# Two blocks of an output projection put into a hand-written order on all queues, and two copies out of banks moved forward

## The chip, the core and the metric

The kernel runs on one core of one Trainium2 chip. It is one layer of a diffusion transformer, launched once. The metric is the device time of one launch in microseconds (us), lower is better. The time before is the median of three runs. In the text PE is the matrix engine, ACT the scalar engine, DVE the vector engine, POOL the engine that here adds squares and issues a few transfers, and SP the engine whose queue issues nearly all loads.

## What is computed

512 latent tokens and 256 context tokens of width 2048 pass one layer: modulated RMSNorm, one input projection, eight heads of differential attention and eight of latent attention, one output projection, and a gated MLP of width 5632 whose gate passes a convolution of width 3. What matters here, cut from the reference:

```python
mod_x = (silu(c) @ w_ada + b_ada)               # 6 x 2048 numbers for the whole sequence
sh1, s1, g1, sh2, s2, g2 = split(mod_x, 6)
x = x + g1 * (merge_heads(o_da, o_mla) @ w_o)    # output projection, 2048 x 2048
h2 = rmsnorm(x, norm2_w) * (1 + s2) + sh2
g, u = split(h2 @ w_up, 2)
x = x + g2 * ((silu(conv3(g)) * u) @ w_down)
return rmsnorm(x, final_w)
```

## The kernel before, in words

Everything is kept transposed: a tile has 128 features on the partitions and 512 tokens along the free axis. Products keep near float32 accuracy from fast matmuls by splitting each operand into a high and a low part. A weight block of 128x1024 is loaded by SP into a buffer `wr` (a ring of three). ACT casts it to the high part `wh` (line 250 in `split`, or line 1740 in `cast`), and DVE subtracts that from the raw block to get the low part `wl` (line 251, or line 1748 in `low`). `wh` and `wl` are rings of three as well. One product is then three matmuls (`mm3`, lines 286 to 288): high by high, high by low, low by high. The first two need only `wh`; the third needs `wl`.

**The output projection** makes 16 feature tiles in four groups of four. Each group runs over eight weight blocks `w_o[g, kb]`, and each block feeds 24 matmuls of 512 columns (`project`, line 1409). The four groups:

- Group 0 (the first block) belongs to an order of steps that a planner wrote for attention (`ATTENTION_ORDER`). It sums into two double banks `s`. One weight block of group 1 is prepared there too (`first_blocks`, line 1438).
- Groups 1 and 2 (the second and third block) are the loop of lines 1493 to 1511. It is written outside any hand-ordered region, so the framework's own scheduler decides the order on every queue. Group 1 sums into four banks `b`, group 2 into the double banks `s`.
- Group 3 is the list of jobs `("o", kb)` (`last_projection`, line 1770), inside a hand-ordered region. There PE, ACT, DVE and SP execute exactly in the order in which the program names their instructions.

When a group ends, each of its four sums is closed: DVE multiplies it by g1 and adds the residual (`gated`, line 1490; `residual`, line 1482, loads the residual tile `xr`, a ring of four, and reserves the result), POOL issues the write of the result to DRAM (line 1510), ACT squares it (line 1463 or 1466, `sq` with two buffers), and POOL adds the square to the running sum `ss` (line 1467), which the second RMSNorm needs. In a group's last weight block the matmuls are sorted by output, so that the four sums become complete one after the other.

**The late part of the modulation** is worked off beside the projection. 22 columns of `modx` are still to be made. For each, a row of 128x2048 floats (1 MB) of `w_ada` is loaded into `ada` (two buffers), and DVE multiplies it with silu(c), which lies broadcast in `cb`, and sums along the row (line 354 in `gemv`, line 1766 in `late_gate`; called a gate below). Sixteen gates belong to groups 1 and 2, one for each weight block; six belong to the jobs of group 3. `late_row` (line 1757) loads the row, `late_gate` works it off and calls `late_row` for the next one.

**After the projection** come the sum of squares over partitions (PE, lines 1823 and 1826 in `last_projection`) and the norm, then the up projection: three tiles computed plainly (jobs `n` and `u`) and 41 tiles by Strassen's method in seven products each (jobs `("p", ft, k)`, `product`, line 1929; the first such tile is ft = 3). Down projection blocks (`d`) are put between them later on. For every job i, `strassen` issues the matmuls, then `cast(i + 2)` on ACT, then `after(jobs[i - 1])`, then `low(i + 2)` on DVE.

In a Strassen tile the seven products are summed in three banks `y`, `z`, `x`. `y` is read in between: product 0 is copied out (`kept`, line 1682, an ACT copy into a ring `m` of two buffers; called m1), product 2 is then added in the same bank and copied as u2, and so is `z` after product 3 (m5). A product that adds to a bank has to wait until the copy of the bank's earlier state is done. `m` has two buffers, so m5 needs m1 to have been used up; that is done by the gate half's `put_together` (lines 1687 and 1688, DVE). In the tile before, the convolution (lines 1660 and 1662), Silu (line 1667), the product with u (line 1671) and the split into parts (lines 1673 and 1677) are finished during this tile's products.

Of the kernel before, what the change touches and what calls it, by code (L numbers as in the profile page):

```python
# [9 lines left out]
F32 = mybir.dt.float32  # L10
# [212 lines left out]
def layer_kernel(ctx: ExitStack, tc: tile.TileContext, small, rope, c_row, cc_row, x_t, ctx_t, ada, ada_k,  # L223
# [15 lines left out]
    def s_tile():  # L239
        return ps_s.tile([P, 1024], F32, tag="s", name=nm("s"))  # L240
# [3 lines left out]
    def b_tile(tag="b", bufs=None):  # L244
        return ps_b.tile([P, 512], F32, tag=tag, name=nm(tag), bufs=bufs or nb[0])
# [29 lines left out]
    def wblock(src):  # L275
        return wsplit(wload(src))
# [466 lines left out]
    def next_gemv(pool, count):  # L743
        for _ in range(count):
            j = next(gv, None)
            if j is not None:
                gemv(pool, j, [(cb, modx)])
# [661 lines left out]
    def project(outs, i, kt, w, stop=False):  # L1409
        o = (kt % 2) * 512 + i * P  # L1410
        mm3(outs[i], (w[0][:, o:o + P], w[1][:, o:o + P]), osp[kt], kt == 0, kt == 15 or stop)
# [44 lines left out]
    tp = tc.alloc_tile_pool(name="tp", bufs=8, reuse_waits="tile")  # L1456
    wo = tc.alloc_tile_pool(name="wo", bufs=1, reuse_waits="tile")
    cb = wo.tile([P, D], F32, name="cb2")
    nc.sync.dma_start(cb, silu_c.to_broadcast([P, D]))

    def add_square(pool, ss, x, first):
        if first:
            sc.square(ss, x)
        else:
            q = pool.tile([P, T], F32, tag="sq", name=nm("sq"), bufs=2)[:, :x.shape[1]]
            sc.square(q, x)
            gp.tensor_tensor(out=ss, in0=ss, in1=q, op=ALU.add)
# [14 lines left out]
    def residual(dt):  # L1482
        xr = wo.tile([P, T], F32, tag="xr", name=nm("xr"), bufs=4)
        nc.sync.dma_start(xr, x_t[dt])
        x1.append(b2k())
        return xr

    def gated(dt, po, xr, c=slice(0, T)):

        ve.scalar_tensor_tensor(out=x1[dt][:, c], in0=po[:, c], scalar=modx[:, 32 + dt:33 + dt], in1=xr[:, c],  # L1490
                                op0=ALU.mult, op1=ALU.add)

    for g in range(3):
        if g % 2:
            outs = [b_tile() for _ in range(4)]
        elif g:
            s0, s1 = s_tile(), s_tile()
            outs = [s0[:, :512], s0[:, 512:], s1[:, :512], s1[:, 512:]]
        else:
            outs = g0_outs  # L1500
        for kb in range(8 if g else 0):
            next_gemv(wo, 1)
            w = g1_first.pop(0) if g1_first else wblock(w_o[g, kb])
            order = [(j, i) for j in range(2) for i in range(4)]
            for j, i in sorted(order, key=lambda t: t[1]) if kb == 7 else order:
                project(outs, i, kb * 2 + j, w)
        for i in range(4):
            dt = g * 4 + i
            gated(dt, outs[i], residual(dt))
            gp.dma_start(x1_d[dt], x1[dt])  # L1510
            add_square(wo, ss, x1[dt], dt == 0)

    KBS = [kb for j in range(4) for kb in (j, j + 4)]
    jobs = [("o", kb) for kb in range(8)] + [("n", kb) for kb in KBS] + [("u", b) for b in range(4)]
# [157 lines left out]
    def kept(src):  # L1680
        t = mem["mm"].tile([P, T], F32, tag="m", name=nm("m"), bufs=2)
        sc.copy(t, src)
        return t
# [80 lines left out]
    def late_gate():  # L1764
# [2 lines left out]
                                scalar=col("b_ada", j), accum_out=modx[:, j:j + 1])  # L1767
        late_row()

    def last_projection(i):  # L1770
        kb, w = jobs[i][1], [h[0] for h in ready[i][:2]]
        if kb < 6:
# [169 lines left out]
    def output_block(c, w):  # L1942
        live["po"] = []
        for d in range(2):
# [2 lines left out]
                mm3(po, w[f * 2 + d], acts[c * FC + f], f == 0, f == FC - 1)  # L1947
            live["po"].append(po)

    def after(job):  # L1950

        if job == ("u", 3):
            live[2] = {"g": live["s"][0], "u": live["s"][1], "t": gate_in(2, live["s"][0])}
        elif job[0] == "d":
            for d, po in enumerate(live["po"]):
                dt = job[2] * 2 + d
                x = mem["mm"].tile([P, T], F32, tag="xs", name=nm("xs"), bufs=XS)
                sc.mul(x, po, modx[:, 80 + dt:81 + dt])  # L1958
                gp.dma_start(x1_d[dt], x, accum_op=ALU.add)  # L1959
        if job[0] != "p":  # L1960
            return
        ft, k = job[1:]
        v, f = live[ft], live.get(ft - 1)
        if k == 0:
            v["m1"] = kept(v["y"])
        elif k == 2:
            v["u2"] = kept(v["y"])
            if f:
                silu(convolve(ft - 1, f["g"], f["t"]))
        elif k == 3:  # L1970
            if f:
                acts[ft - 1] = multiply(f["t"], f["u"])
            v["g"] = mem["mm"].tile([P, T], F32, tag="g", name=nm("g"), bufs=1)
            put_together(v["g"][:, h0], v["x"], v["m1"])
            v["m5"] = kept(v["z"])
        elif k == 4:
            if f:
                finish(f["t"], acts[ft - 1])
            v["u"] = mem["mm"].tile([P, T], F32, tag="u", name=nm("u"), bufs=1)
            put_together(v["u"][:, h1], v["y"], v["m5"])  # L1980
        elif k == 5:
            put_together(v["u"][:, h0], v["z"], v["u2"])
        elif k == 6:
            v["t"] = gate_in(ft, v["g"])
# [8 lines left out]
    def strassen(i):  # L1993
        job = jobs[i]
        if job[0] == "p":
            ft, k = job[1:]
            product(ft, k, weights(i))
            if k in (1, 2) or (k == 0 and ft > 3):
                weight_sum(ft, k + 2)
            elif k == 6:  # L2000
                weight_sum(ft + 1, 1)
            if (ft, k) == (NFT - 1, 1):
                for dt in range(KT):
                    x1[dt] = a2k()
                    nc.sync.dma_start(x1[dt], x1_d[dt])
            if ft == 3 and k < 2:
                fill(len(queue) if k else 4)
        else:
            output_block(job[1], weights(i))
        second_gate(jobs[i - 1])  # L2010
        cast(i + 2)
        after(jobs[i - 1])
        low(i + 2)


# [106 lines left out]

    with tc.manual_schedule(engines={mybir.EngineType.PE, mybir.EngineType.Activation, mybir.EngineType.DVE,
                                     mybir.EngineType.SP}):
        mem["ra"] = Ring(wp, "wr", 3, items_a)
        live["o"] = [b_tile() for _ in range(4)]
        live["xr"] = [residual(12 + d) for d in range(4)]
        ve.tensor_tensor(db, modx[:, 56:64], modx[:, 48:56], op=ALU.add)
        late_row()
        late_row()  # L2130
        for i in range(2):
            cast(i)
            low(i)
        for i, job in enumerate(jobs):
            if job == ("n", 0):
                ps_b.release()
                ps_s.release()
                nb[0] = 3
                ps_b = tc.alloc_tile_pool(name="ps_m", bufs=3, space=PSUM, reuse_waits="tile")
                spare += [tp.tile([P, T], F32R, tag="tp", name=nm("tp")) for _ in range(8)]  # L2140
            {"o": last_projection, "n": first_tiles, "u": third_tile, "p": strassen, "d": strassen,
             "f": last_output}[job[0]](i)
# [86 lines left out]
```

## Time and profile before

| | |
|---|---|
| median of three runs | 2338.05 us (2332.84 to 2338.72) |
| profiled execution, its own time | 2336.14 us |
| its span, first to last instruction | 2334.4 us |
| PE busy | 2290.5 us (98%) |
| DVE busy | 1722.1 us (74%) |
| ACT busy | 1164.1 us (50%) |
| mean granted PE clock | 0.993 of full speed |

The profile is of one execution. A row of a timeline says when an instruction started, how long it took, engine, line, operation, what it writes and reads, and in brackets how long the engine sat idle before it and who released it. The row of a DMA on the SP queue is only its issue; landing is told by the views of transfers and of the chain of waits. A matmul of 512 columns is listed with about 0.39 us, but starts follow each other closer than that, since matmuls are pipelined; the distance of the starts is what counts.

### The profile page before, as it was taken

Reading aid. Unit: us, or ns where it says so; the run is one execution under the profiler, and the core shown is the slowest. Engines: PE = TensorE matmul, PEld = TensorE weight load, DVE = VectorE, ACT = ScalarE, POOL = GpSimd, SP = SyncE. Lnnn points to the kernel's source line nnn. Section 1 sums busy time; section 2 is a strip of 40 time slices with the busy share of each in tenths; the row PEclk is TensorE's granted clock in tenths of the full one; section 3 lists DMA queues with packets and bytes.
Section 4 is the critical chain, followed back from the end, with each engine's and each line's share of the span. In section 5 each row is a group of like instructions: output and inputs, shape, how many; then the busy total and the mean of one; then the engine's idle time right before and its main releaser. Section 6 shows DMA issues by size and latency. Waiting matters only on the chain.

```text
span 2334.4 us, 32178 instructions
## 1 busy us (share of the span) xinstructions
PE 2290.5 (98%) x12378; PEld 1960.0 (84%) x12378; DVE 1722.1 (74%) x2206; ACT 1164.1 (50%) x1777; POOL 266.2 (11%) x308
## 2 busy tenths in 40 slices
PE   6999999999999999999999999999999999999998
PEld 5788888888888878898888888888888888888887
DVE  7988785689877575897675858585858585867667
ACT  6542311577777522455454545454545454545455
POOL 0000001200133131000101010101010101010110
PEclk8999999999999999999999999999999999999999
DMA  9978888546210298434646473646464555555573
GB/s 367 370 254 306 302 305 298 168 135 203 81 34 28 93 353 293 155 120 129 140 137 151 111 169 109 171 111 155 132 147 130 139 136 144 136 146 125 156 184 103
DMA packets 124731, 404.23 MB, mean 173 GB/s; under 512 B 14337, under 2 KB 18945, under 8 KB 114081
## 3 DMA queue, kind: packets, MB, share of 16 engines
q1 hardware_dynamic: 96658, 346.92, 44.4%
q0 software_dynamic: 26768, 54.21, 12.6%
q8 instruction: 97, 1.59, 0.3%
q10 hardware_dynamic: 1152, 1.05, 0.1%
q14 instruction: 56, 0.46, 0.1%
HBM read 332.45 MB, written 69.67 MB: 172 GB/s over the span
## 4 chain that ended last, share of the span: by engine, by line
PE 90%; DMA 4%; DVE 3%; issue 1%; ACT 1%; SPq 0%; POOL 0%; DVEq 0%; ACTq 0%; POOLq 0%
PE y L1938 13%; PE b L286 10%; PE b L287 9%; PE b L288 9%; PE y L1940 7%; PE z L1938 6%; PE s L1025 4%; PE z L1940 3%; PE s L286 3%; PE s L288 3%; PE x L1938 3%; PE s L287 3%; DMA ada<-in_ada 2%; PE pt L1045 2%; PE f L286 2%; PE f L288 2%
## 5 line engine op out<-in xcount | busy, mean ns | idle before, releaser
L1748 DVE TENSOR_TENSOR wl<-wr,wh 128x1024 fp32r<-128x1024 f32 x144 | 176.5, 1226 | 139.5 <-ACT wh L1740 138.8
L1959 POOL DMA_DIRECT2D x_d<-xs x160 | 139.6, 993 | 1148.3 <-ACT xs L1958 1146.3
L1740 ACT CAST wh<-wr 128x1024 fp32r<-128x1024 f32 x144 | 150.9, 1048 | 218.4 <-PE b L287 113.2
L286 PE MATMUL b<-ah,wh 128*128 128x512 f32 (+1 forms) x664 | 256.8, 387 | 0.0
L287 PE MATMUL b<-al,wh 128*128 128x512 f32 (+1 forms) x664 | 256.7, 387 | 0.0
L288 PE MATMUL b<-ah,wl 128*128 128x512 f32 (+1 forms) x664 | 255.8, 385 | 0.0
L1748 DVE TENSOR_TENSOR wl<-rb,wh 128x1024 fp32r<-128x1024 f32 x123 | 150.0, 1220 | 120.7 <-ACT wh L1740 120.7
L1748 DVE TENSOR_TENSOR wl<-ws,wh 128x1024 fp32r<-128x1024 f32 x123 | 150.3, 1222 | 110.1 <-ACT wh L1740 110.1
L1740 ACT CAST wh<-rb 128x1024 fp32r<-128x1024 f32 x123 | 129.3, 1051 | 175.1 <-PE b L287 80.1
L1938 PE MATMUL y<-a2k,wh 128*128 128x512 f32 x656 | 164.0, 392 | 0.0
L1740 ACT CAST wh<-ws 128x1024 fp32r<-128x1024 f32 x123 | 128.4, 1044 | 69.7 <-PE b L287 44.1
L288 PEld LDWEIGHTS b<-ah,wl 128*128 128x128 f32 x664 | 124.8, 188 | 25.7
L286 PEld LDWEIGHTS b<-ah,wh 128*128 128x128 f32 x664 | 125.1, 188 | 22.9
L287 PEld LDWEIGHTS b<-al,wh 128*128 128x128 f32 x664 | 125.1, 188 | 21.9
L250 ACT CAST wh<-wr 128x1024 fp32r<-128x1024 f32 x51 | 53.5, 1052 | 171.6 <-DMA wr<-in_w_o 45.2
L1938 PEld LDWEIGHTS y<-a2k,wh 128*128 128x128 f32 x656 | 118.6, 189 | 21.6
L354 DVE CUSTOM_DVE_ANT_0 ada<-ada,cb,smt 128x2048 f32<-128x2048 f32 x37 | 88.2, 2388 | 30.3 <-DMA ada<-in_ada 30.1
L1938 PE MATMUL y<-b2k,wh 128*128 128x512 f32 x410 | 106.8, 390 | 0.0
L1958 ACT ACTIVATE xs<-b,modx 128x512 f32<-128x512 f32 x160 | 101.7, 681 | 6.2 <-DMA x_d<-xs 6.2
L1030 ACT ACTIVATE p<-s,m 128x768 f32<-128x768 f32 x96 | 86.6, 903 | 30.8 <-DVE m L1028 28.7
L1028 DVE TENSOR_REDUCE m<-s 128x1 f32<-128x768 f32 x96 | 90.6, 950 | 6.9 <-PE s L1025 6.5
L1940 PEld LDWEIGHTS y<-a2k,wl 128*128 128x128 f32 x656 | 89.5, 190 | 6.4
(530 smaller groups left out, 5934.8 us busy)
## 6 DMA issues: line engine op xcount, KB each, us to landing
ada<-in_ada SPq DMA_DIRECT2D x80, 1024.0 KB, 7.2
rb<-in_w_up SPq DMA_DIRECT2D x123, 512.0 KB, 4.4
wr<-in_w_dn SPq DMA_DIRECT2D x88, 512.0 KB, 3.8
x_d<-xs POOLq DMA_DIRECT2D x160, 256.0 KB, 6.0
wr<-in_w_up SPq DMA_DIRECT2D x53, 512.0 KB, 4.3
wr<-in_w_f SPq DMA_DIRECT2D x34, 512.0 KB, 6.0
adak<-in_ada_k SPq DMA_DIRECT2D x32, 512.0 KB, 7.6
wr<-in_w_o SPq DMA_DIRECT2D x32, 512.0 KB, 7.1
```

Of the source, the lines that this page charges most:

```text
L286: pe.matmul(out, st[0], mv[0], start=start, stop=False, **kw)
L287: pe.matmul(out, st[0], mv[1], start=False, stop=False, **kw)
L288: pe.matmul(out, st[1], mv[0], start=False, stop=stop, **kw)
L354: ve.tensor_tensor_reduce(out=junk, in0=w, in1=vec, op0=ALU.mult, op1=ALU.add, scale=1.0, scalar=col("b_ada", j), accum_out=dst[:, j:j + 1])
L1025: pe.matmul(s()[:, c0:c1], a, b[:, c0:c1], start=i == 0, stop=i == len(ms) - 1)
L1028: step("DVE", 0.87, t + cost + 0.2, lambda: ve.tensor_reduce(out=m(), in_=s()[:, :TT], axis=AX.X, op=ALU.max, negate=True), r=[s], w=[m])
L1740: sc.copy(t, raw[:, k * n_:k * n_ + n_])
L1748: ve.tensor_tensor(t, raw[:, k * n_:k * n_ + n_], hi[k].bitcast(F32), op=ALU.subtract)
L1938: pe.matmul(o, w[j][0], hs[j], start=start and j == 0, stop=False, skip_group_check=True)
L1940: pe.matmul(o[:, h0], w[j][1], hs[j][:, h0], start=False, stop=j == 7, skip_group_check=True)
L1958: sc.mul(x, po, modx[:, 80 + dt:81 + dt])
L1959: gp.dma_start(x1_d[dt], x, accum_op=ALU.add)
```

## The change

It has three edits.

1. The loop over groups 0 to 2 and the load of `cb` are taken out of the automatically ordered part. A function `middle_blocks` does the same work inside the hand-ordered region, where it is called first. It names the order for PE, ACT, DVE and SP; POOL's order stays automatic.
2. The jobs' ring of weight buffers (`mem["ra"]`, which starts its loads when it is made) is made inside `middle_blocks` at block 13 of 16; the first two rows of the late modulation are loaded at its start; the first job's split is done at block 15.
3. In the first Strassen tile, the copy of `y` after product 0 goes ahead of the cast of two jobs later, and the `put_together` of the gate half and the copy of `z` come one job earlier, ahead of the convolution and Silu of the tile before. The other tiles keep their order.

```diff
     cb = wo.tile([P, D], F32, name="cb2")
-    nc.sync.dma_start(cb, silu_c.to_broadcast([P, D]))
...
-    for g in range(3):
-        if g % 2:
-            outs = [b_tile() for _ in range(4)]
...
-        for kb in range(8 if g else 0):
-            next_gemv(wo, 1)
-            w = g1_first.pop(0) if g1_first else wblock(w_o[g, kb])
-            order = [(j, i) for j in range(2) for i in range(4)]
-            for j, i in sorted(order, key=lambda t: t[1]) if kb == 7 else order:
-                project(outs, i, kb * 2 + j, w)
-        for i in range(4):
-            dt = g * 4 + i
-            gated(dt, outs[i], residual(dt))
-            gp.dma_start(x1_d[dt], x1[dt])
-            add_square(wo, ss, x1[dt], dt == 0)
...
+    def middle_blocks():
+
+        blocks = [(g, kb) for g in (1, 2) for kb in range(8)]
+        ready_w, raws, coming = list(g1_first), [], iter(blocks[1:])
+
+        def load_block():
+            b = next(coming, None)
+            if b:
+                raws.append(wload(w_o[b[0], b[1]]))
+
+        def close(g, outs, xr):
+            for i in range(4):
+                dt = g * 4 + i
+                gated(dt, outs[i], xr[i])
+                gp.dma_start(x1_d[dt], x1[dt])
+                add_square(wo, ss, x1[dt], dt == 0)
+
+        load_block()
+        load_block()
+        nc.sync.dma_start(cb, silu_c.to_broadcast([P, D]))
+        outs, xr = g0_outs, [residual(i) for i in range(4)]
+        late_row()
+        late_row()
+        for s, (g, kb) in enumerate(blocks):
+            load_block()
+            if kb == 0:
+                before = outs, xr
+                if g == 1:
+                    outs = [b_tile() for _ in range(4)]
+                else:
+                    s0, s1 = s_tile(), s_tile()
+                    outs = [s0[:, :512], s0[:, 512:], s1[:, :512], s1[:, 512:]]
+            w = ready_w.pop(0)
+            order = [(j, i) for j in range(2) for i in range(4)]
+            for j, i in sorted(order, key=lambda t: t[1]) if kb == 7 else order:
+                project(outs, i, kb * 2 + j, w)
+            if raws:
+                ready_w.append(wsplit(raws.pop(0)))
+            else:
+                cast(0)
+                low(0)
+            if kb == 0:
+                close(g - 1, *before)
+            if s == 13:
+                mem["ra"] = Ring(wp, "wr", 3, items_a)
+            if kb == 3:
+                xr = [residual(g * 4 + i) for i in range(4)]
+            late_gate()
+        close(2, outs, xr)
...
+    def first_gate(v):
+        v["g"] = mem["mm"].tile([P, T], F32, tag="g", name=nm("g"), bufs=1)
+        put_together(v["g"][:, h0], v["x"], v["m1"])
+
     def after(job):
...
         elif k == 2:
             v["u2"] = kept(v["y"])
+            if ft == 3:
+                first_gate(v)
+                v["m5"] = kept(v["z"])
             if f:
                 silu(convolve(ft - 1, f["g"], f["t"]))
         elif k == 3:
             if f:
                 acts[ft - 1] = multiply(f["t"], f["u"])
-            v["g"] = mem["mm"].tile([P, T], F32, tag="g", name=nm("g"), bufs=1)
-            put_together(v["g"][:, h0], v["x"], v["m1"])
-            v["m5"] = kept(v["z"])
+            if ft > 3:
+                first_gate(v)
+                v["m5"] = kept(v["z"])
...
         second_gate(jobs[i - 1])
-        cast(i + 2)
-        after(jobs[i - 1])
+        if job == ("p", 3, 1):
+            after(jobs[i - 1])
+            cast(i + 2)
+        else:
+            cast(i + 2)
+            after(jobs[i - 1])
         low(i + 2)
...
-        mem["ra"] = Ring(wp, "wr", 3, items_a)
+        middle_blocks()
         live["o"] = [b_tile() for _ in range(4)]
         live["xr"] = [residual(12 + d) for d in range(4)]
         ve.tensor_tensor(db, modx[:, 56:64], modx[:, 48:56], op=ALU.add)
-        late_row()
-        late_row()
-        for i in range(2):
-            cast(i)
-            low(i)
+        cast(1)
+        low(1)
```

More of the change, by code (lines that the diff above doesn't have):

```diff
@@ L1491, in gated @@
                                 op0=ALU.mult, op1=ALU.add)
-    for g in range(3):
-        if g % 2:
-            outs = [b_tile() for _ in range(4)]
[L1496 to L1500, printed above, removed]
-        for kb in range(8 if g else 0):
-            next_gemv(wo, 1)
-            w = g1_first.pop(0) if g1_first else wblock(w_o[g, kb])
-            order = [(j, i) for j in range(2) for i in range(4)]
-            for j, i in sorted(order, key=lambda t: t[1]) if kb == 7 else order:
-                project(outs, i, kb * 2 + j, w)
-        for i in range(4):
-            dt = g * 4 + i
-            gated(dt, outs[i], residual(dt))
-            gp.dma_start(x1_d[dt], x1[dt])
-            add_square(wo, ss, x1[dt], dt == 0)
     KBS = [kb for j in range(4) for kb in (j, j + 4)]
```

## The prediction

> **What bounds the kernel now.** I read the page, then PE's waits, then the two stretches of time that the change touches. The page's first line:
>
> ```profile
> span 2334.4 us, 32178 instructions
> ```
>
> The execution's own time is 2336.14 us, so 1.7 us lie around the span. PE is busy for nearly all of it, so a gain can only be time in which PE waits or runs at a lower clock. PE's waits from 812 to 965 us, from the end of group 0 to the norm:
>
> ```profile
> PE s L286 <- ACT wh L250: 2.8, 1, 2.8
> ...
> PE s L288 <- DVE wl L251: 1.4, 1, 1.4
> ...
> PE s L1823 <- POOL ss L1810: 1.0, 1, 1.0
> PE b L288 <- DVE wl L1748: 0.2, 1, 0.2
> ```
>
> PE's timeline shows where the first two are. The rows are the first matmul of group 1, the last of group 1, four of group 2 and the first of group 3:
>
> ```profile
> 818.37 0.39 PE L286 MATMUL b<-a2k,wh 128*128 128x512 f32 x1
> ...
> 861.66 0.39 PE L288 MATMUL b<-a2k,wl 128*128 128x512 f32 x1
> 864.88 0.50 PE L286 MATMUL s<-a2k,wh 128*128 128x512 f32 x1 [2.83 <-ACT wh L250]
> ...
> 867.50 0.79 PE L288 MATMUL s<-a2k,wl 128*128 128x512 f32 x1 [1.42 <-DVE wl L251]
> ...
> 873.63 0.42 PE L286 MATMUL s<-a2k,wh 128*128 128x512 f32 x1
> ...
> 913.15 0.39 PE L286 MATMUL b<-a2k,wh 128*128 128x512 f32 x1
> ```
>
> Group 1 runs densely: 192 starts, so (861.66 - 818.37) / 191 = 0.2266 us from start to start, 5.44 us for a weight block. Group 2 begins with a hole, waits again for the low part, and then starts 14 matmuls in 6.13 us (867.50 to 873.63), where 3.17 would do. The stretches by clock say why:
>
> ```profile
> 870.00:880.00 10.00, 10.00 (x37) 8.03 (x37) 9.05 (x9) 2.84 (x3) 1.86 (x1) 0.82 1.01 409
> ```
>
> After the hole the granted clock is 0.82 in the mean, and the transfer engines are full (share 1.01, 409 GB/s). Who made the block late is seen on SP's queue, in the chain of waits and on DVE:
>
> ```profile
> 847.92 4.55 SPq L351 DMA_DIRECT2D ada<-in_ada  x2
> 852.53 2.11 SPq L1484 DMA_DIRECT2D xr<-in_x_t  x4
> 855.79 0.33 SPq L351 DMA_DIRECT2D ada<-in_ada  x1
> 856.22 0.39 SPq L259 DMA_DIRECT2D wr<-in_w_o  x1
> ```
> ```profile
> 832.65 7.48 DMA ada<-in_ada
> ...
> 856.22 7.47 DMA wr<-in_w_o
> ...
> 941.79 6.93 DMA ada<-in_ada
> ```
> ```profile
> 866.22 1.22 DVE L251 TENSOR_TENSOR wl<-wr,wh 128x1024 fp32r<-128x1024 f32 x1
> ```
>
> Block 8 (group 2's first) is issued only at 856.22, behind two rows, four residuals and another row, each row waiting for a gate to free its buffer. It lands at 863.69. PE wanted it cast at 861.89.
>
> **Part 1, groups 1 and 2 in written order.** No matmul, cast, gate or byte is added or taken away. What moves is SP's order: now a block's load (three ahead), then one row (two ahead), in strict turn. Block 8's load is named in step 5, behind row 6, which waits for gate 4. That gate is due one block time per step after gate 0, some 30 us before block 8 is used. So the hole goes if nothing else is late. I check the deadlines in the new order.
>
> DVE now does, per step s: low part of block s+1, gate s. So the low part of block s+2 stands behind gate s, and SP's next row behind it too. At the start:
>
> ```profile
> 812.90 0.42 SPq L1459 DMA_DIRECT2D cb<-silu_c  x1
> ...
> 815.38 0.96 SPq L351 DMA_DIRECT2D ada<-in_ada  x2
> ```
> ```profile
> 826.97 3.38 DVE L354 CUSTOM_DVE_ANT_0 ada<-ada,cb,smt 128x2048 f32<-128x2048 f32 x1
> ```
> ```profile
> DMA to landing us min/median/max: 5.3/7.1/8.8
> ```
>
> The last row is for the rows of `ada` from 812 to 913 us. The slowest, 8.8, on the first row gives a landing at 824.2; gate 0 ends at most 3.38 later (827.6), block 2's low part 1.22 after that, at 828.8. PE needs it for the third matmul of block 2, at 818.37 + 2 x 5.44 + 0.45 = 829.7. It holds, by 0.9 us at the worst. Later steps have more room: a row buffer's cycle is landing 7.1 + gate 2.35 (row at 948.85, below) + issue 0.33 = 9.8 us for two steps, where PE takes 10.9. At a group's end DVE stands at the closing until PE has finished; queued behind it are gate 8 and block 10's low part, due only 10.9 us later. At the end of group 2 the margin is smallest: the cast and low part of job 1 stand behind close(2) on ACT and DVE, and PE wants them 5.44 us after the end of group 2. The pieces:
>
> ```profile
> 821.35 0.63 ACT L1463 ACTIVATE ss<-b2k 128x512 f32<-128x512 f32 x1 [1.95 <-DVE b2k L1490]
> ...
> 869.69 1.04 ACT L250 CAST wh<-wr 128x1024 fp32r<-128x1024 f32 x1 [2.66 <-DMA wr<-in_w_o]
> ```
> ```profile
> 952.26 1.40 DVE L1490 SCALAR_TENSOR_TENSOR b2k<-b,modx,xr 128x512 f32<-128x512 f32 x2
> ```
>
> The first three sums are closed while PE finishes the fourth, so behind the end lie one gating (0.7), one square (0.6), a cast (1.04) and a low part (1.22): 3.6 us of 5.44. No stall is forecast. All 384 matmuls then take 384 x 0.2266 = 87.0 us instead of 913.15 - 818.37 = 94.8: **-7.7 us**, of which 2.96 is the lower clock (6.13 - 3.17) and the rest the two waits and the ramp.
>
> Here the Trainium skill ("TensorE: Matmul & The Clock Gate", "What's actually happening") puts the half clock after an idle window of about 3.4 us and ends it after one busy window of the same length. By it the slow stretch would cost 1.7 instead of 2.96, and the part would be worth about 6.5. The trace's slow stretch is 6.13 us, and its own count of starts decides.
>
> Two rows of the modulation are now loaded before group 3, where before they came with a crowd at its start. So PE's wait of 0.2 us (line 1748) goes: **-0.2 us**. And the six last gates come earlier. Before, the last one held up the first closing of group 3:
>
> ```profile
> 948.85 2.35 DVE L1766 CUSTOM_DVE_ANT_0 ada<-ada,cb,smt 128x2048 f32<-128x2048 f32 x1 [1.86 <-DMA ada<-in_ada]
> ```
> ```profile
> 955.71 1.28 POOL L1810 TENSOR_TENSOR ss<-ss,sq 128x512 f32<-128x512 f32 x1
> ```
> ```profile
> 957.04 1.12 PE L1823 MATMUL s<-ss,ones 128*128 128x512 f32 x2 [0.99 <-POOL ss L1810]
> ```
>
> Its row was issued at 941.79 and landed at 948.72. With rows 16 and 17 there at the start, gates are paced by `wl` buffers that PE frees each 5.44 us, and gate 21 falls about 32 us after group 3's first matmul, not 38 (948.85 + 2.35 - 913.15). The first sum of group 3 is complete at 6 x 5.44 + 12 x 0.2266 = 35.4 us after that start; before, it was closed at 952.26, 39.1 after. POOL's second addition then ends near 41.2 (second sum complete at 38.1, gating 0.7, square 0.6, addition 1.3, and 0.5 for semaphores), and PE reaches line 1823 at 42.3. The 1.0 us of waiting goes with its 0.1 of restart: **-1.1 us**. Next late is ACT's last square, as before.
>
> **Part 2, the Strassen tile.** Two waits are aimed at, the first two rows here; the last two rows are the same products of the next tile:
>
> ```profile
> 1040.88 0.97 PE L1938 MATMUL y<-tp,wh 128*128 128x512 f32 x3 [0.57 <-ACT m L1682]
> ...
> 1050.66 0.73 PE L1938 MATMUL z<-tp,wh 128*128 128x512 f32 x2 [1.12 <-ACT m L1682]
> ...
> 1061.94 0.86 PE L1938 MATMUL y<-tp,wh 128*128 128x512 f32 x3
> ...
> 1070.32 0.65 PE L1938 MATMUL z<-tp,wh 128*128 128x512 f32 x2
> ```
> ```profile
> 1061.03 0.57 ACT L1682 COPY m<-y 128x512 f32<-128x512 f32 x1
> ...
> 1069.60 0.59 ACT L1682 COPY m<-z 128x512 f32<-128x512 f32 x1 [0.49 <-PE y L1938]
> ```
> ```profile
> 1038.50:1058.60 20.10, 18.41 (x104) 15.83 (x103) 19.96 (x26) 10.24 (x15) 0.00 (x0) 1.00 0.32 105
> ```
>
> Both waits go: the first copy loses the cast (1.04) ahead of it, the second its `put_together` and a Silu. But DVE is busy for 19.96 of 20.1 us there; the edit only reorders it, and it ends when it did. ACT's casts hang on it, so the copy of the next tile ends at 1061.60 as before. PE, 1.7 us earlier, would want it at 1060.25 and must wait until 1061.66 (0.06 from a copy's end to the matmul, an estimate from 1070.19 and 1070.32, which are 0.13 apart with no wait). 0.28 us is left. At 1070.32 the copy ends at 1070.19, and 0.07 is left. So **-0.1 us**; bounds: -1.7 if DVE's chain moves up, +0.5 if the later Silu delays a cast.
>
> Sum: -7.7 - 0.2 - 1.1 - 0.1 = **-9.1 us**, so 2327.0 on the profiled execution. The runs' median is 1.9 above that: 2338.05 - 9.1 = **2328.9**.
>
> **Rivals.**
> - *Strassen's waits stay gone.* For it: the reorder takes 1 us of `put_together` out of a later job. Against: DVE's full row. 9.1 + 1.6 = 10.7 less, 2327.3.
> - *A new wait at the start.* If row 0 lands so late that gate 0 starts at 826.97 as now and takes 3.38, block 2's low part ends at 831.6, 1.9 after PE's 829.7. Alone that leaves -7.2 (2330.8); with a slow clock like the 2.96 above, -4.2 (2333.8). Against it: DVE did another low part (1.2) ahead of gate 0, and block 3's load went ahead of the rows.
> - *The transfers are the bound.* Gate 13 must end 1.22 before block 15's low part is due at 818.37 + 15 x 5.44 + 0.45 = 900.4, so it starts by 896.9. Up to it SP brings, from 812.9 on, `cb`, 14 rows, 12 residuals and 13 blocks (24.5 times 1024 KB), and POOL writes 2 times that: 27.8 MB in 84 us, 331 GB/s. The quoted stretch moved 409. At 300 GB/s it takes 92.7 us and 8.7 are lost: no change, 2337.6. The point is 331.
> - *Slower: the row ring starves PE.* Each row's load now strictly waits for the gate two steps before, and the next block's low part and load stand behind that gate. From a landing of 10.88 - 2.35 - 0.33 = 8.2 us on, each step loses half the excess. With 16 steps and 1 us of margin it eats all 9.1 at 9.5 us; at 10.5 us it costs 18.4 - 1 = 17.4, so 8 us slower, 2346. Against: median 7.1, largest 8.8.
>
> **Numbers.** Chances: forecast 0.62, Strassen too 0.10, new wait 0.15, transfers 0.07, row ring 0.06. A measurement of this kernel can tell about 0.3%, 7.0 us, from no change; the forecast lies 2.1 beyond, while the runs spread over 5.9. Faster by more: 0.51 of the forecast's 0.62, 0.09 of the second, 0.03 of the third, 0.63. Same 0.31, slower 0.06. Range: low 2336.14 - 10.7 - 2.9 (half the spread) = 2322.5; high 2333.8 plus about 1.2 of scatter, 2335.
>
> **What would show it.** Right: SP's rows alternate `wr` and `ada` from 816 us on; group 3 starts near 905.4; no stretch there below clock 0.95; line 1823 no longer waits for POOL; in the Strassen stage PE's two waits are gone and a new one of about 1.4 us stands at the third product of tile 4. Wrong: PE waiting for `wh` or `wl` in the first three blocks or in job 1, rows landing later than 8.2 us, or the Strassen tiles ending 1.6 us earlier beside the norm.

## The result, and the profile after

The kernel after the change takes 2327.76 us (median of 5 runs, 2326.62 to 2329.33). Beside it the kernel before took 2338.05 us (5 runs, 2332.84 to 2341.36). The ratio is 0.9962, interval [0.9945, 0.9978]: 0.38% faster, with an interval that reaches from 0.2% to 0.55%. The forecast was 2328.9 us. The kernel before was run again beside the experiments, with medians of 2336.53 us (22 runs), 2335.73 (12) and 2335.18 (17), 7.4 to 8.8 us above the median after; so the 10.3 us here are at the upper end.

The profiled execution after has a time of its own of 2327.76 us:

```profile
span 2326.0 us, 32180 instructions
```

So 8.4 us of span are gone between the two profiles. Where they went is read from the first matmuls of each stage on PE's timeline, which for the three groups are now:

```profile
819.46 0.39 PE L286 MATMUL b<-a2k,wh 128*128 128x512 f32 x1
...
862.97 0.39 PE L286 MATMUL s<-a2k,wh 128*128 128x512 f32 x1
...
906.49 0.39 PE L286 MATMUL b<-a2k,wh 128*128 128x512 f32 x1
```

| stage | before, us | after, us | difference | forecast |
|---|---|---|---|---|
| up to group 1 (same code) | 818.37 | 819.46 | +1.09 | 0 |
| groups 1 and 2 | 94.78 | 87.03 | -7.75 | -7.7 |
| group 3 to the norm's first matmul | 51.11 | 49.35 | -1.76 | -1.3 |
| norm to the first Strassen tile | 70.31 | 70.31 | 0 | 0 |
| first to third Strassen tile | 41.37 | 41.43 | +0.06 | -0.1 |
| the rest | 1258.46 | 1258.42 | -0.04 | 0 |

The first row is scatter. In the twelve kernels that were run besides, group 1 starts between 817.02 and 821.68 us, although the code ahead of it is the same. The rest of the table is the change.

Groups 1 and 2 run without a hole. The stretch in windows (after the bounds: its length, then busy time of PE, PEld, DVE, ACT and POOL with the number of instructions, then clock, transfer share and GB/s), PE's waits from 812 to 965 us, and SP's queue at the start:

```profile
812.00:906.00 94.00, 94.00 (x416) 77.86 (x415) 70.47 (x60) 23.19 (x27) 18.12 (x17) 1.00 0.94 352
```
```profile
PE b L286 <- DVE n L1856: 1.7, 1, 1.7
PE s L1847 <- ACT sq L1811: 1.0, 1, 1.0
PE b L286 <- ACT a2k L1568: 0.3, 1, 0.3
```
```profile
824.74 0.33 SPq L1732 DMA_DIRECT2D ada<-in_ada  x1
825.15 0.38 SPq L259 DMA_DIRECT2D wr<-in_w_o  x1
830.26 0.33 SPq L1732 DMA_DIRECT2D ada<-in_ada  x1
```

PE is busy for all of the 94 us at full clock, and rows and blocks alternate on SP. The three waits that are left belong to the norm and were there before. The waits for `wh`, `wl` and for POOL are gone. The transfers carry 352 GB/s through the stretch, and PE waits for none of them; they were no limit.

In the Strassen stage the two old waits are gone and two others have come (product 6 of the first tile, product 2 of the second), 1.61 us together, where the old ones were 1.69:

```profile
1044.06 2.08 PE L1959 MATMUL y<-a2k,wh 128*128 128x512 f32 x8 [0.99 <-ACT wh L1711]
...
1053.29 0.97 PE L1959 MATMUL y<-tp,wh 128*128 128x512 f32 x3 [0.62 <-ACT m L1653]
```

### The profile page after: what moved, and what is told of

It reads as the page before. It is cut to its first block, busy times and chain, and to the rows that moved or that the text cites. A ratio compares the mean times of both kernels' runs of the same rounds, so it can differ in the third digit from the quotient of the medians.

```text
span 2326.0 us, 32180 instructions
## 1 busy us (share of the span) xinstructions
PE 2287.8 (98%) x12378; PEld 1959.2 (84%) x12378; DVE 1726.0 (74%) x2206; ACT 1164.4 (50%) x1777; POOL 266.0 (11%) x308
## 4 chain that ended last, share of the span: by engine, by line
PE 95%; DVE 3%; ACT 1%; DMA 1%; issue 1%; SPq 0%; POOL 0%; DVEq 0%; ACTq 0%
PE y L1959 13%; PE b L286 11%; PE b L287 11%; PE b L288 11%; PE y L1961 7%; PE z L1959 6%; PE s L1025 4%; PE s L286 3%; PE s L287 3%; PE s L288 3%; PE z L1961 3%; PE x L1959 3%; PE pt L1045 2%; PE f L286 2%; PE f L287 2%; PE f L288 2%
## 5 line engine op out<-in xcount | busy, mean ns | idle before, releaser
L1961 PE MATMUL y<-a2k,wl 128*128 128x256 f32 x656 | 91.5, 282 | 0.0
```

Of the source, the lines that this page charges most:

```text
L1961: pe.matmul(o[:, h0], w[j][1], hs[j][:, h0], start=False, stop=j == 7, skip_group_check=True)
```

## The experiments

All durations by stage are differences of first matmuls, as in the table. "The mid stage" is groups 1 and 2.

**The two parts alone.** `mid_only` takes the third edit back, `strassen_only` is the kernel before with the third edit alone. The core of the two diffs, against after and against before:

```diff
-            if ft == 3:
-                first_gate(v)
-                v["m5"] = kept(v["z"])
...
-        if job == ("p", 3, 1):
-            after(jobs[i - 1])
-            cast(i + 2)
-        else:
-            cast(i + 2)
-            after(jobs[i - 1])
+        cast(i + 2)
+        after(jobs[i - 1])
```
```diff
+            if ft == 3:
+                first_gate(v)
+                v["m5"] = kept(v["z"])
...
+        if job == ("p", 3, 1):
+            after(jobs[i - 1])
+            cast(i + 2)
+        else:
+            cast(i + 2)
+            after(jobs[i - 1])
```

> The written order of the middle blocks alone, with the Strassen tile in its old order. Theory: the whole gain is here, since the Strassen edit only moves a wait: about 0.996 of before (9 us less), groups 1 and 2 in 87.0 us as after (94.8 before), group 3 to the norm in 49.4 (51.1 before), first to third Strassen tile 41.4 with the two old waits of 0.6 and 1.1 back. Rival (the Strassen edit gives its 1.7 us): 1.7 us slower than after, 41.4 against 39.7 in that stretch.

> The Strassen edit alone on the kernel before. Theory: no change that can be measured (within 0.1 us in its stretch, 41.4 us from the first product of tile 3 to that of tile 5); the two waits for copies go, and waits of the same sum stand at product 6 of tile 3, where VectorE has not yet read bank y, and at product 2 of tile 4. Rival: 1.7 us faster, the stretch in 39.7.

`mid_only` took 2329.05 us (10 runs, 2326.48 to 2331.17), ratio to before 0.9967 [0.9956, 0.9978]. `strassen_only` took 2333.91 us (12 runs, 2331.64 to 2339.26), ratio 0.9992 [0.9982, 1.0003]. The kernel before, beside both, had 2336.53 us (22 runs, 2330.92 to 2344.26). So the gain belongs to the written order. By stages, `mid_only` has 87.04 us in the mid stage, 49.34 from group 3 to the norm, and the two old Strassen waits again in a stretch of 41.36 us:

```profile
1030.83 0.96 PE L1959 MATMUL y<-tp,wh 128*128 128x512 f32 x3 [0.57 <-ACT m L1653]
...
1040.60 0.74 PE L1959 MATMUL z<-tp,wh 128*128 128x512 f32 x2 [1.12 <-ACT m L1653]
```

`strassen_only` has 51.40 us from group 3 to the norm, 41.43 in the Strassen stretch, and a surprise in the mid stage: 90.55 us, with the same automatic order for which the profile before shows 94.78. Its timeline and windows at the start of group 2:

```profile
863.78 0.50 PE L286 MATMUL s<-a2k,wh 128*128 128x512 f32 x1 [0.30 <-ACT wh L250]
...
867.05 0.50 PE L288 MATMUL s<-a2k,wl 128*128 128x512 f32 x1 [2.07 <-DVE wl L251]
```
```profile
860.00:870.00 10.00, 7.63 (x33) 5.68 (x32) 9.39 (x8) 4.63 (x6) 9.44 (x8) 1.00 1.01 373
```

The hole is there again, but it is shorter, and the clock column says 1.00: the matmuls behind it are not slow. SP's loads come in the same order in both profiles. So the automatic order pays for the hole in both, but not the same price: 3.5 us and 7.75 us over the 87.0 of dense matmuls.

**Bringing the hole back in the written order.** In `block8_late` the loads of blocks 8 and 9 wait for gate 6, in `block8_later` those of blocks 8 to 10 wait for gate 7, which for that goes ahead of the split of block 8. The two diffs against after:

```diff
-            load_block()
+            if s not in (5, 6):
+                load_block()
...
             late_gate()
+            if s == 6:
+                load_block()
+                load_block()
```
```diff
-            load_block()
+            if s not in (5, 6, 7):
+                load_block()
...
+            if s == 7:
+                late_gate()
+                for _ in range(3):
+                    load_block()
...
-            late_gate()
+            if s != 7:
+                late_gate()
```

> After, with one load moved: block 8, the first of group 2, is loaded behind gate 6 and the row that waits for it, two steps later than written, at about 855 us instead of 845; nothing else changes. Theory (the place of that load in SP's order made the hole): it lands about 862, is cast by 863.5 and PE, which wants it at 863.0, waits 0.5 to 2.5 us with no fall of the clock, so groups 1 and 2 take 87.5 to 89.5 us. Rival (the order on VectorE and ScalarE, or the rate of all transfers, made it): 87.0 as after.

> After, with the load of block 8 (the first of group 2) held back behind gate 7, three loads then in a row. Theory (the old order lost its time because this one load stood behind rows in SP's queue): it is issued near 859.5, lands near 866, so group 2 starts 4 to 5 us late, TensorE then has a stretch at a lower clock as in before (2.5 to 3 us more), and groups 1 and 2 take 93 to 96 us instead of 87.0. Rival (the order of the loads matters little; the transfers are what limits): 87 to 89 us. Without the lower clock behind the hole: 91 to 92 us.

`block8_late` (one run, 2328.79 us) needs 88.74 us for the mid stage. That is the time expected, but at another place: block 8 still comes in time, and PE waits 0.41 us for `wh` and 0.56 for `wl` of block 10. `block8_later` (one run, 2333.91 us) needs 94.18 us, and its start of group 2 looks like that of the kernel before:

```profile
866.05 0.79 PE L286 MATMUL s<-a2k,wh 128*128 128x512 f32 x1 [3.92 <-ACT wh L250]
...
867.31 0.79 PE L288 MATMUL s<-a2k,wl 128*128 128x512 f32 x1
...
871.74 0.46 PE L286 MATMUL s<-a2k,wh 128*128 128x512 f32 x1
```
```profile
860.00:870.00 10.00, 6.04 (x18) 4.09 (x17) 3.95 (x5) 2.81 (x4) 0.54 (x1) 0.75 0.79 305
870.00:880.00 10.00, 10.00 (x42) 8.16 (x41) 7.23 (x6) 3.70 (x5) 8.64 (x8) 0.91 0.65 227
```

Loads that come too late at this one place are enough for the whole loss: a wait of 3.92 us, then 12 starts in 5.69 us (866.05 to 871.74) where 2.72 would do, so 2.97 us of lower clock. The profile before had 2.96. The rival, that transfers are the limit whatever their order, is out.

**One buffer for the rows.** This asks what the row ring is worth, and so the price of the slower rival. Against after:

```diff
-            w = wo.tile([P, D], F32, tag="ada", name=nm("ada"), bufs=2)
+            w = wo.tile([P, D], F32, tag="ada", name=nm("ada"), bufs=1)
...
         late_row()
-        late_row()
```

> After, with one buffer for the modulation rows instead of two, so that each row is requested only when the gate before it has ended. Theory (the rows' landing is covered by the second buffer): a step then takes issue 0.33 + landing 5.5 to 7.3 + gate 2.35 us = 8.2 to 10 us instead of 5.44, block by block, for some 20 steps less the slack: 40 to 75 us slower, with slow clock stretches on top. Rival (gates are off TensorE's path and the blocks' low parts go around them): under 5 us.

It took 2378.32 us (one run), 50.6 us more than after: 24.4 in the mid stage (111.44 us) and 23.8 from group 3 to the sum of squares (66.05 instead of 42.24). The timeline of DVE shows a gate each 7.2 to 9.1 us, mostly 7.2 to 7.6, always waiting for its row, and the chain of waits in that stretch is one row after the other:

```profile
834.25 2.35 DVE L1737 CUSTOM_DVE_ANT_0 ada<-ada,cb,smt 128x2048 f32<-128x2048 f32 x1 [3.22 <-DMA ada<-in_ada]
841.41 2.35 DVE L1737 CUSTOM_DVE_ANT_0 ada<-ada,cb,smt 128x2048 f32<-128x2048 f32 x1 [3.67 <-DMA ada<-in_ada]
848.71 2.35 DVE L1737 CUSTOM_DVE_ANT_0 ada<-ada,cb,smt 128x2048 f32<-128x2048 f32 x1 [3.80 <-DMA ada<-in_ada]
```
```profile
836.63 4.64 DMA ada<-in_ada
...
843.80 4.78 DMA ada<-in_ada
```

The mechanism of the slower rival is real: with gates, low parts and loads in one strict order, a gate that waits for its row holds PE. With two buffers it does not get that far. With no other row on its way a row lands in 4.9 us in the median here (4.6 to 8.2), so most steps are 7.3 us and not the 8.2 to 10 of the expectation, where the crowded landings of after had been used.

**What removed the wait for POOL at the sum of squares.** The prediction says: the two rows that are now loaded before group 3. `rows_late` loads them behind the residuals of group 3, where they were before. `weights_late` leaves the rows early and holds back the other load that has moved, the fourth of the jobs' ring (the weight block of job 3). `rows_weights_late` does both. The edits, against after:

```diff
-    def late_gate():
+    def late_gate(more=True):
...
-        late_row()
+        if more:
+            late_row()
...
-            late_gate()
+            late_gate(s < 14)
...
         ve.tensor_tensor(db, modx[:, 56:64], modx[:, 48:56], op=ALU.add)
+        late_row()
+        late_row()
```
```diff
-                mem["ra"] = Ring(wp, "wr", 3, items_a)
+                mem["ra"] = Ring(wp, "wr", 3, items_a[:3])
...
         ve.tensor_tensor(db, modx[:, 56:64], modx[:, 48:56], op=ALU.add)
+        mem["ra"].items = items_a
+        mem["ra"].pump()
```

> After, with one part undone: the two rows of the modulation that are there when group 3 begins are loaded only at its start, behind the residuals, as before. Theory: groups 1 and 2 stay at 87.0 us; the last gate ends about 38 us after the first matmul of group 3 instead of 34.5, the first sum is closed late, PE waits about 1 us for POOL at the sum of squares again, and group 3 to the norm goes back from 49.4 towards 51.1 us. Rival (the gain there came with the denser stage ahead of it): it stays at 49.4.

> The same kernel as rows_late, since that run lost 4.9 us at a place that the edit does not touch. If the wait of 2.2 us at job 1 was the landing of one modulation row in that one run, it is gone here: groups 1 and 2 at 87.0, group 3 to the sum of squares 42.3 to 43.5 us with the wait at L1845 back at 0 to 1.1 us, and times near 2328 to 2330. If it belongs to the edit, the wait at job 1 is here again, group 3 to the sum of squares is near 47 us and the median near 2335.

> After, with the fourth load of the jobs' ring (the weight block of job 3) held back until the residuals of group 3 have been issued; the two rows stay early. In after it was issued at 897.9, 8.6 us before group 3; here it comes near 2 us behind its start. rows_late_again took the rows away from the early place and the wait at the sum of squares did not come back, so the rows were not what removed it. Theory (it was job 3's weights: in before they landed 14.5 us into group 3, job 3's low part stood between two gates on VectorE and so the gates came late): the low part of job 3 comes 3 to 6 us later than in after, and as in before the last gate ends 36 to 38.3 us after group 3's first matmul instead of 34.5; TensorE's wait for GpSimd at the sum of squares is back in part or whole, group 3 to that line 42.3 to 43.9 us. Rival (either early rows or early weights are enough): last gate near 34.5, no wait, 42.24 us.

> After, with both: the two rows and the load of job 3's weights behind the residuals of group 3, which is the order of loads that before has at this place. Theory (the loads' order alone makes the wait, wherever the blocks before were placed): last gate 38 us after group 3's first matmul, TensorE waits 1.0 us for GpSimd at the sum of squares, group 3 to that line 43.9 us, to the norm 51 us. Rival (something else of the written order removed it): 42.24 us and no wait.

| kernel | last gate ends, after group 3's first matmul | wait for POOL | group 3 to the sum of squares |
|---|---|---|---|
| before | 38.1 | 0.99 | 43.89 |
| after | 34.5 | 0 | 42.24 |
| rows_late_again | 34.7 | 0 | 42.26 |
| weights_late | 32.0 | 0 | 42.45 |
| rows_weights_late | 38.6 | 1.99 | 44.37 |

`rows_late` itself lost 4.9 us elsewhere (next part), so its times say nothing here; `rows_late_again` is the same kernel run anew (2328.95 us, 6 runs, 2328.46 to 2330.13). The other two were run once each, 2328.70 and 2331.22 us. My theory for `weights_late` fell too: either load may come late, and the wait returns only when both do. On POOL's and PE's timelines of `rows_weights_late`:

```profile
950.73 1.27 POOL L1832 TENSOR_TENSOR ss<-ss,sq 128x512 f32<-128x512 f32 x1
```
```profile
952.05 1.13 PE L1845 MATMUL s<-ss,ones 128*128 128x512 f32 x2 [1.99 <-POOL ss L1832]
```

How both together do it is seen on DVE, first in `rows_weights_late` and then in after:

```profile
917.99 2.35 DVE L1737 CUSTOM_DVE_ANT_0 ada<-ada,cb,smt 128x2048 f32<-128x2048 f32 x1 [2.94 <-DMA ada<-in_ada]
...
922.82 1.23 DVE L1719 TENSOR_TENSOR wl<-wr,wh 128x1024 fp32r<-128x1024 f32 x1 [2.47 <-ACT wh L1711]
923.97 2.35 DVE L1737 CUSTOM_DVE_ANT_0 ada<-ada,cb,smt 128x2048 f32<-128x2048 f32 x1
```
```profile
913.79 2.34 DVE L1737 CUSTOM_DVE_ANT_0 ada<-ada,cb,smt 128x2048 f32<-128x2048 f32 x1
...
916.06 1.22 DVE L1719 TENSOR_TENSOR wl<-wr,wh 128x1024 fp32r<-128x1024 f32 x1
917.20 2.34 DVE L1737 CUSTOM_DVE_ANT_0 ada<-ada,cb,smt 128x2048 f32<-128x2048 f32 x1
```

Between the first two gates of group 3 stands job 3's low part. With both loads late, the first gate waits for its row (2.94), and then the low part waits for ACT's cast (2.47), which itself had waited for the weights until 921.74. The two waits follow one another. With one of them early, the later gates catch up before the end of the group.

**The thin margin at job 1.** The run of `rows_late` (2335.02 us) lost its time at a place that its edit does not touch. The last gate of group 2 ended late, and behind it on DVE stand the four closings and job 1's low part:

```profile
906.16 2.35 DVE L1737 CUSTOM_DVE_ANT_0 ada<-ada,cb,smt 128x2048 f32<-128x2048 f32 x1 [4.31 <-DMA ada<-in_ada]
...
908.43 2.73 DVE L1489 SCALAR_TENSOR_TENSOR b2k<-s,modx,xr 128x512 f32<-128x512 f32 x4
```
```profile
914.81 0.50 PE L286 MATMUL b<-a2k,wh 128*128 128x512 f32 x1 [2.21 <-ACT wh L1711]
...
916.10 0.79 PE L288 MATMUL b<-a2k,wl 128*128 128x512 f32 x1 [0.55 <-DVE wl L1719]
```

PE then runs at a lower clock (0.83 in the window from 910 to 920 us), and group 3 to the sum of squares takes 47.10 us. The kernel `job1_first` writes job 1's cast and low part ahead of the closings:

```diff
             late_gate()
+        cast(1)
+        low(1)
         close(2, outs, xr)
...
         ve.tensor_tensor(db, modx[:, 56:64], modx[:, 48:56], op=ALU.add)
-        cast(1)
-        low(1)
```

> After, with job 1's cast and low part written ahead of the closing of group 2 instead of behind it. In the profile of rows_late the last gate of group 2 ended at 908.5, 1.5 us behind group 3's due start (907.0), and job 1's cast and low part, queued behind four closings on VectorE and four squares on ScalarE, made TensorE wait 2.21 and 0.55 us with a slow stretch behind it; group 3 up to the sum of squares took 47.1 us instead of 42.2. Theory (the last gate of group 2 sets the end of a thin margin): with the move job 1's low part follows that gate directly, and no wait at job 1 comes even where the gate is as late; the closing is one low part (1.2 us) later, which nobody waits for; a calm run is as after (2326.6 to 2329.3), and the runs scatter no more than after's. Rival (the closing is what counts): the first banks come free 1.2 us later and the sum of squares with them, 0 to 1.2 us slower, and any late run is as late as before.

By chance its profiled execution had the late gate too:

```profile
906.21 2.35 DVE L1737 CUSTOM_DVE_ANT_0 ada<-ada,cb,smt 128x2048 f32<-128x2048 f32 x1 [3.69 <-DMA ada<-in_ada]
...
908.49 1.22 DVE L1719 TENSOR_TENSOR wl<-wr,wh 128x1024 fp32r<-128x1024 f32 x1
909.62 2.72 DVE L1489 SCALAR_TENSOR_TENSOR b2k<-s,modx,xr 128x512 f32<-128x512 f32 x4
```

The gate ends 1.0 us behind group 3's first matmul (908.56 and 907.54), and PE does not wait at all: 42.24 us to the sum of squares. The other profiles give the scale. The gate ends 2.9 us before group 3's first matmul in after, without a wait. In `block8_late` it is 0.35 before, with waits of 0.36 and 0.56 us; in `rows_late` 1.5 behind, with 2.21 and 0.55. The other profiles with this order and two row buffers have 1.65 (`weights_late`) to 4.1 us, none with a wait at job 1. So the latest end that costs nothing lies between 0.35 and 1.65 us before group 3 is due, and an execution in which a row lands late pays. The times of `job1_first`, 2329.20 us (6 runs, 2326.88 to 2329.85; ratio 0.9967 [0.9955, 0.9979]), cannot be told from after's.

**What sets the Strassen tile's pace.** `fewer_dve_new` leaves two of DVE's four weight differences out for that tile; `pool_sums` computes all and gives those two to POOL. Against after:

```diff
-            ve.tensor_tensor(w12, w22, w12, op=ALU.subtract)
+            if ft > 3:
+                ve.tensor_tensor(w12, w22, w12, op=ALU.subtract)
...
-            ve.tensor_tensor(sums_[ft, 2], w21, sums_[ft, 2], op=ALU.subtract)
+            if ft > 3:
+                ve.tensor_tensor(sums_[ft, 2], w21, sums_[ft, 2], op=ALU.subtract)
```
```diff
-            ve.tensor_tensor(w12, w22, w12, op=ALU.subtract)
+            (gp if ft == 3 else ve).tensor_tensor(out=w12, in0=w22, in1=w12, op=ALU.subtract)
...
-            ve.tensor_tensor(sums_[ft, 2], w21, sums_[ft, 2], op=ALU.subtract)
+            (gp if ft == 3 else ve).tensor_tensor(out=sums_[ft, 2], in0=w21, in1=sums_[ft, 2], op=ALU.subtract)
```

> After, leaving out two of the weight differences that VectorE makes for the first Strassen tile (the third and fourth of that tile; 1.22 us each, 1.14 from start to start), so two of its seven products are made with weights that are not the difference. Theory (VectorE sets that tile's pace, and the two copies moved forward only moved the waits): both waits of TensorE in the tile and the next (0.99 and 0.62 us) are gone or under 0.3, and the stretch from the tile's first product to the third tile's first is 39.8 to 40.2 us instead of 41.43. Rival (ScalarE's casts set the pace, or the banks' copies): the waits stay within 0.3 us of where they are, 41.1 to 41.5 us.

> After, with the same two weight differences made by GpSimd instead of VectorE, all computed. If VectorE sets the pace of the tile and its 2.3 us come free: the two waits go and the stretch is 39.8 to 40.2 us, 1.2 to 1.6 us faster than after. Rival (a GpSimd operation beside VectorE slows it: beside GpSimd's additions a low part took 2.29 us instead of 1.22 and a gate 3.38 instead of 2.35, so two operations of some 2.6 us give back about 2 us): 41.0 to 41.6 us, no gain. If a product waits for a difference that GpSimd makes late, a new wait stands there.

`fewer_dve_new` (one run, 2326.83 us): both waits are gone, the stretch takes 39.57 us instead of 41.43. So DVE sets the pace, and moving copies can't shorten the tile. `pool_sums` took 2330.32 us (12 runs, 2328.40 to 2334.32; ratio 0.9978 [0.9969, 0.9986]). Its interval overlaps that of after (0.9945 to 0.9978), so the stretch decides: it takes 43.57 us, slower than after and than both expectations, with new waits:

```profile
1033.23 0.96 PE L1959 MATMUL y<-tp,wh 128*128 128x512 f32 x3 [1.77 <-ACT m L1653]
...
1035.97 0.79 PE L1959 MATMUL y<-b2k,wh 128*128 128x512 f32 x1 [0.46 <-DVE b2k L1575]
```

Their reason stands on two engines' timelines:

```profile
1033.07 2.56 POOL L1680 TENSOR_TENSOR ws<-rb,ws 128x1024 f32<-128x1024 f32 x1 [10.75 <-DVE wl L1719]
```
```profile
1032.90 0.48 DVE L1575 SCALAR_TENSOR_TENSOR a2k<-h,db,a2k 128x256 fp32r<-128x256 f32 x1
1033.30 2.62 DVE L1575 SCALAR_TENSOR_TENSOR b2k<-h,modx,b2k 128x256 fp32r<-128x256 f32 x1
```

The same DVE instruction takes 0.48 us alone and 2.62 beside POOL: it ends 0.3 us after POOL does. Two such stalls of 2.1 us cost DVE more than the 2.3 us that it was relieved of. PE's waits alone are only 0.6 us more than after's (2.23 against 1.61). Most of the rest of the 2.14 us is a lower clock: 0.83 in the mean from 1030 to 1040 us, where after has 1.00. The Trainium skill ("GPSIMD Engine Reference", "Key points") says that POOL shares its memory interfaces with DVE and that DVE instructions with two inputs from there suffer; the row agrees and gives the size.

No version that does the whole work beat the kernel after the change by more than the scatter of its runs.

## Why the prediction was right, and where it was not

**Groups 1 and 2, -7.7: measured -7.75.** The mechanism (block 8's load too late on SP, a hole, a slow stretch) is shown by `block8_later`, which makes it again by holding back that load and the next two. The size holds against the one execution that was profiled. `strassen_only` shows an execution in which the same order loses 3.5 us and the clock does not fall, so "2.96 is the lower clock" is not paid in every run. The medians carry less of it: `mid_only` is 2336.53 - 2329.05 = 7.5 us below before, and with the 1.76 of group 3 that leaves about 5.7 for this part. That the forecast used a profile that had paid the full price, and not one like that of `strassen_only`, was luck.

**The deadlines.** Block 2's low part ended at 826.9, due at 830.8 (819.46 + 2 x 5.44 + 0.45): it held. The step "behind the end lie ... 3.6 us of 5.44" was too kind in two places. It takes the first three sums as closed while PE finishes the fourth. But the third and the fourth are the halves of one double bank, and DVE closes both only when PE is done with that bank. The operation that makes `db` follows, and by the profile ACT's last square waits for it:

```profile
906.70 1.41 DVE L1489 SCALAR_TENSOR_TENSOR b2k<-s,modx,xr 128x512 f32<-128x512 f32 x2 [1.31 <-PE s L288]
908.02 0.73 DVE L2160 TENSOR_TENSOR db<-modx 128x8 f32<-128x8 f32 x1
```
```profile
908.75 0.63 ACT L1465 ACTIVATE sq<-b2k 128x512 f32<-128x512 f32 x1 [0.57 <-DVE db L2160]
```

So in after job 1's low part starts at 910.35, takes 1.2 and ends 5.1 us behind group 3's first matmul, not 3.6. By the prediction's count (5.44) 0.4 us is left where it had 1.8; PE needs the low part only at its third matmul, at 912.4 (906.49 + 5.44 + 0.45), 0.8 us later. The step also leaves out the gate that DVE has to finish before any closing, and so the row that the gate waits for. In after that gate ended in time; in `rows_late` it did not, and made a loss of 4.9 us. The price is shown; how often it comes is not: among the eleven profiles with the written order and two row buffers, the gate was that late in three (`rows_late`, `job1_first`, and `block8_late`, which itself holds loads back).

**The start of group 3, -0.2, and the sum of squares, -1.1: measured -1.76 together.** Where PE reaches the line was right to 0.1 us (42.24 after the start of group 3, forecast 42.3), and so was the first complete sum (closed at 35.6, forecast 35.4). The reason given was half of it: "with rows 16 and 17 there at the start" the gates come earlier, but `rows_late_again` has them early without that, because job 3's weights had also moved ahead, and the prediction did not list them as moved. And the gates are not "paced by `wl` buffers": in after the last one ends at 34.5 and not 32, because rows are waited for:

```profile
934.92 2.35 DVE L1737 CUSTOM_DVE_ANT_0 ada<-ada,cb,smt 128x2048 f32<-128x2048 f32 x1 [3.46 <-DMA ada<-in_ada]
938.61 2.35 DVE L1737 CUSTOM_DVE_ANT_0 ada<-ada,cb,smt 128x2048 f32<-128x2048 f32 x1 [0.19 <-DMA ada<-in_ada]
```

It was enough all the same, since the first sum is complete only at 35.4. The waits themselves were 1.2 us. Another 0.3 is the slower starts right at them (distances of 0.56, 0.34 and 1.27 us where 0.23 would do, 1.5 in all), 0.1 lies behind the sum of squares, and the remaining 0.2 is open.

**The Strassen tile, -0.1: measured +0.06.** That DVE sets the end is shown by `fewer_dve_new`. The waits come back with 1.61 us where about 1.4 was said, but 0.99 of it three products earlier than named, in the tile before. Product 6 adds to bank `y`, and in after DVE is still reading that bank:

```profile
1043.23 0.68 DVE L1658 TENSOR_TENSOR m<-y,m 128x512 f32<-128x512 f32 x1
```

It ends at 1043.91, and PE starts at 1044.06; the distance is 0.15 to 0.16 us in eight profiles with this wait. The profile's row names ACT's cast, which ends just when PE starts but belongs to a product of the next tile. That the reader of `y` is the cause is read from this order and from `fewer_dve_new`; no run takes that reader alone away. It was not in the prediction's list.

**The rivals.** Strassen's waits did not stay gone. Block 2's low part had 3.9 us to spare, so there was no new wait at the start. The transfers moved 352 GB/s over the stretch, above the 331 that was needed, and 409 from 882 to 892 us. The row ring did not starve PE, though `one_row_buffer` shows what it would look like.

**The median.** 1.1 us below the forecast, within the scatter of the runs. The spans of the two profiles are 8.4 us apart, where 9.1 was forecast: the stages with a forecast gave 9.45, and 1.09 went the other way by scatter ahead of group 1.

## What to carry to other kernels

When a load arrives too late, look for what stands ahead of it in the issuing queue, and count the price of the hole twice: the wait, and the slow matmuls behind it, which come in some executions and not in others. When checking a deadline in a strict order, write down every instruction ahead of the one that is due, on its own engine and behind every wait of those: here one gate and its row were left out, and that is where the time was lost when it was lost. Where an engine is busy for the whole stretch, moving its instructions moves the waits; only taking work from it helps, and here not by handing that work to POOL, which stalled DVE meanwhile.

## What the runs showed of the hardware

How much waiting brings the clock down is not settled by these runs. In `rows_late` PE waited 2.21 and 0.55 us with two matmuls between them, 3.5 us in all (912.61 to 916.10); the granted clock was 0.50 from 916 to 919 us, and the matmuls started 0.43 us apart until 919.25. In `pool_sums` PE had waited 1.77 us in one piece and then worked again for 1.3 us (from 1033.23) when the clock fell: it was 1.00 up to 1034.5 and about 0.5 from there to 1037.9. In `strassen_only` PE waited 0.30 and 2.07 us with four matmuls between them, 3.6 us in all (863.48 to 867.05), and nothing slowed down. The Trainium skill ("TensorE: Matmul & The Clock Gate", "What's actually happening") names an idle window of about 3.4 us that runs freely; here less idle time than that was enough in two runs and not in a third. Three cases don't settle the rule.

Once down, the clock stays down for different lengths: about 3.4 us in `pool_sums` (1034.5 to 1037.9) and in `rows_late` (915.9 to 919.3), about 6.8 us in the profile before (866.8 to 873.7) and in `block8_later` (865.0 to 871.9). Where it was 6.8, PE was still waiting when the clock fell and went on waiting for 0.7 and 1.0 us; in `rows_late` that was 0.2.
